# Down projection in two passes by halves of the features, with seven-product Strassen blocks for five of 32 K tile pairs per pass

## The chip, the cores and the metric

The kernel runs on one core of one Trainium2 chip. The metric is the device time of one execution in microseconds. A core has five engines that work beside each other, each with its own queue of instructions: TensorE (PE in the profile; PEld is its load of the stationary operand), VectorE (DVE), ScalarE (ACT), GpSimd (POOL) and SyncE (SP, which only issues DMAs here).

## The reference

One layer of a hybrid encoder block, 256 tokens of 2048 features in float32, one batch. The part that the change touches is the last line but one.

```python
proj = x @ w_in[l]
...
mix = jnp.concatenate([ret_out, mla_out], axis=-1) @ w_out[l]
x = _layer_norm(DEEPNORM_ALPHA * x + mix, ln1_g[l], ln1_b[l])
h = jnp.square(jax.nn.relu(x @ w_up[l])) @ w_down[l]     # (256, 8192) @ (8192, 2048)
x = _layer_norm(DEEPNORM_ALPHA * x + h, ln2_g[l], ln2_b[l])
```

## The kernel before

All large products keep float32 accuracy by splitting each operand into a high part, rounded to the type float32r, and a low part, the rest, and by three matmuls: high by high, high by low, low by high. For the weights, ACT casts the high part (L175) and DVE subtracts it for the low part (L176), 128x1024 elements at a time; such a piece is called a half tile here.

The weights come in `Job`s, in the order in which they are used: a load of 1 MB into one of three `raw` buffers (`NRAW`, on SP's queue) and pieces that split it into one of five slots (`NSLOT`). `unit()` is called after each group of matmuls and writes up to two further pieces into the queues of ACT and DVE (`next_piece`), as long as the slot five pieces back has been given back by `free`. A piece without a slot (`slotted` false) goes out as soon as its turn comes. The order in every queue is the order of these calls, as `manual_schedule` is set: nothing is reordered. Generators in `side` are stepped once per unit, ahead of the pieces.

The up projection goes over 64 feature tiles; `up_evac` squares the positive part into `rr` (8192 x 256, transposed, in SBUF). The down projection is `xstat`: the tokens are the stationary operand (two blocks `tb` of 128), the weights stream 512 columns at a time. Before the change its loop (L937 to L949) goes over K tiles `kt` of 128; all 2048 features of both token blocks accumulate in the eight PSUM banks `ad`. A K tile is 2 (token blocks) x 3 (parts) x 4 (banks) = 24 matmuls. `r_split(b)` makes high and low part of `rr` for four K tiles at a time (block b), into two buffers `rhl`, in the middle of the block before (L946). Two `row_job`s (ln1's gain and bias, `x1_piece`, L351) stand between the weights after K tiles 8 and 16; `last_residual` adds the residual of the last bank by two matmuls with the identity. Six K tiles are held back: four are split ahead into `slab` buffers (`staged_down`), and at the end each bank gets its last 18 matmuls by itself (`down_bank`, L976 to L991), while DVE adds the residual, takes the statistics and finishes the banks before.

Of the kernel before, what the change touches and what calls it, by code (L numbers as in the profile page):

```python
# [14 lines left out]
P = 128  # L15
D = 2048
# [15 lines left out]
HALF_PI = 1.5707963267948966  # L32
PI_LO = 3.1415925
NRAW = 3
NDOWN = 58
NSLOT = 5
X_AFTER = {0: (1, 1), 1: (2, 2), 3: (4, 4), 6: (8, 4), 10: (12, 4)}

# [13 lines left out]
class Job:  # L52


    def __init__(self, load, pieces, slotted):
        self.load = load
        self.pieces = pieces
        self.slotted = slotted
        self.emitted = 0
# [8 lines left out]
def kernel(  # L68
# [32 lines left out]
    def acc(name):  # L101
        return psum.tile([P, 512], F32, tag="acc", name=name)
# [19 lines left out]
    def next_piece(force):  # L122
        while state["job"] < len(jobs) and jobs[state["job"]].emitted == len(jobs[state["job"]].pieces):
            state["job"] += 1
        if state["job"] == len(jobs):
            return False
        job = jobs[state["job"]]
        if job.slotted:
            if len(holders) >= NSLOT and not force and not holders[-NSLOT][0]:
                return False  # L130
            holders.append(job.free[job.emitted])
        load_ahead(state["job"])
        job.pieces[job.emitted]()
        job.emitted += 1
        return True

    def use(job, n=None):
        while job.emitted < (len(job.pieces) if n is None else n):
            next_piece(True)
        return Cols(job.hi, job.width), Cols(job.lo, job.width)  # L140

# [9 lines left out]
    def weights(src, n, name, into=None, width=1024, cuts=None):  # L151

        job = Job(None, [], into is None)
        job.width = width
        spans = list(zip(cuts, cuts[1:])) if cuts else [(0, n)]

        def load():
            raw = raw_tile(job, f"raw_{name}")
            for i, (a, b) in enumerate(spans):
                (nc.scalar if name == "mla0" and i == 0 else nc.sync).dma_start(raw[:, a:b], src[:, a:b])  # L160

        def piece(i):
            a, m = i * width, min(width, n - i * width)
            if into is None:
                hi = wsp.tile([P, 1024], F32R, tag="hi", name=f"hi_{name}_{i}")
                lo = wsp.tile([P, 1024], F32R, tag="lo", name=f"lo_{name}_{i}")
            else:
                hi, lo = into(i)
            job.hi.append(hi)
            job.lo.append(lo)  # L170
            for o, e in spans if cuts else ((a, a + m),):
                o, e = max(o, a) - a, min(e, a + m) - a
                if o < e:
                    r = job.raw[:, a + o:a + e]
                    nc.scalar.copy(hi[:, o:e], r)  # L175
                    nc.vector.tensor_sub(lo[:, o:e], r, hi[:, o:e].bitcast(F32))  # L176
# [145 lines left out]
    def staged_down(i):  # L322
        def into(j):
            if (i // 2, "down") not in staged:
                staged[i // 2, "down"] = slab.tile([P, 8192], F32R, tag="slab", name=f"wst{2 + i // 2}")
            o = (2 * (i % 2) + j) * 2048
            t = staged[i // 2, "down"]
            return t[:, o:o + 1024], t[:, o + 1024:o + 2048]
        return into

    for half in range(2):
        row = []
        for i in range(KT // 2):
# [5 lines left out]
    j_up = [weights(w_up[ft], 2048, f"wu{ft}") for ft in range(64)]  # L339
    norm_rows = {}  # L340

    def row_job(i, pieces):
# [7 lines left out]
        op = nc.vector.tensor_mul if i == 0 else nc.vector.tensor_add  # L350
        op(c, c, norm_rows[i][:, a:a + 1024])  # L351

    down = {}
    for kt in range(NDOWN):
        down[kt] = weights(w_down[kt], 2048, f"wd{kt}")
        if kt in (8, 16):
            i = (8, 16).index(kt)
            row_job(i, [lambda i=i, tb=tb, a=a: x1_piece(i, tb, a) for tb in range(2) for a in (0, 1024)])
        if kt in (36, 41, 46, 51):
            i = (36, 41, 46, 51).index(kt)  # L360
            down[NDOWN + i] = weights(w_down[NDOWN + i], 2048, f"wd{NDOWN + i}", into=staged_down(i))
    for kt in (62, 63):
        down[kt] = weights(w_down[kt], 2048, f"wd{kt}")
    j_down = [down[kt] for kt in range(64)]
    row_job(2, [])
    row_job(3, [])

# [316 lines left out]

    xm = mid.tile([P, 5120], F32, tag="mid", name="xm")
    xt = xm[:, 0:2 * D].rearrange("p (b c) -> p b c", b=2)
    spare = xm[:, 2 * D:].rearrange("p (b i c) -> p b i c", b=2, i=4)
# [3 lines left out]
    def residual(tb, j, pb, st, with_stats=True):  # L691
        c = xt[:, tb, j * 512:(j + 1) * 512]
        if pb is not None:
            nc.vector.scalar_tensor_tensor(c, c, ALPHA, pb, op0=ALU.mult, op1=ALU.add)
        if with_stats:
            nc.vector.bn_stats(st[:, j], c)

    def out_steps(half, i):
        kp = (i + H // 2) % (KT // 2)
# [177 lines left out]

    rr = [slab.tile([P, 32, S], F32, tag="slab", name=f"rr{i}") for i in range(2)]

    def up_evac(ft, pb):  # L880
        t = work.tile([P, S], F32, tag="ut", name="ut", bufs=2)
# [5 lines left out]
    def last_residual(step):  # L887

        if step == 0:
            c = xt[:, 1, 3 * 512:]  # L890
            nc.vector.tensor_copy(identr, ident)
            nc.scalar.activation(mask, ident, AF.Copy, scale=-1.0)
            xb.append(work.tile([P, 2, 512], F32R, tag="xf", name="xb"))
            nc.scalar.activation(xb[0][:, 0], c, AF.Copy, scale=ALPHA)
            nc.vector.scalar_tensor_tensor(xb[0][:, 1], c, ALPHA, xb[0][:, 0].bitcast(F32),
                                           op0=ALU.mult, op1=ALU.subtract)
        else:
            for i in range(2):
                nc.tensor.matmul(ad[1][3], identr, xb[0][:, i], start=False, stop=False)

    xb = []
    rhls = {}

    def r_split(b):
        if b < 16:
            t = work.tile([P, 4, 512], F32R, tag="big", name="rhl", bufs=2)
            r = rr[b // 8][:, b % 8 * 4:b % 8 * 4 + 4]
            nc.scalar.copy(t[:, :, 0:S], r)
            nc.vector.tensor_sub(t[:, :, S:], r, t[:, :, 0:S].bitcast(F32))
            rhls[b] = t  # L910

    for ft in range(NSPLIT):
        up_evac(ft, first_pb[ft])
# [19 lines left out]
            unit()  # L933


    ad = [[(acc if j < 2 else bank)(f"d{tb}{j}") for j in range(4)] for tb in range(2)]
    for kt in range(NDOWN):  # L937
        hi, lo = use(j_down[kt])
        if kt == NDOWN - 2:
            r_split(15)  # L940
        for tb in range(2):
            xstat(ad[tb], [(rhls[kt // 4], kt % 4, hi, lo, 0)], (512,) * 4, kt == 0, False, tb)
            if tb == 1:
                free(j_down[kt])
            unit()
        if kt % 4 == 1 and kt // 4 < 14:  # L946
            r_split(kt // 4 + 1)
        if kt in (32, 36):
            last_residual((kt - 32) // 4)  # L949


    w_staged = []
    for kt in range(NDOWN, 64):
        hi, lo = use(j_down[kt])
        w_staged.append((rhls[kt // 4], kt % 4, hi, lo, 0))
    load_ahead(len(jobs))
    st2 = [stat.tile([P, 4, 6], F32, tag=f"ln{tb}", name=f"lm{tb}", bufs=1) for tb in range(2)]
    g2, b2 = norm_rows[2], norm_rows[3]

    def down_bank(tb, j):  # L960
        xstat(ad[tb], w_staged, (512,) * 4, False, True, tb, banks=(j,))

    def finish(tb, a, b):

# [11 lines left out]
    for j in range(4):  # L976
        down_bank(0, j)
        residual(0, j, ad[0][j], st2[0])
    stats(0, st2[0])

    shift = {j: (acc if j < 2 else bank)(f"sh{j}") for j in (1, 2)}
    for j in range(4):
        down_bank(1, j)
        finish(0, j * 512, (j + 1) * 512)
        if j < 3:
            residual(1, j, ad[1][j], st2[1])
        else:
            nc.vector.bn_stats(st2[1][:, j], ad[1][j])
        if j in shift:
            c = xt[:, 1, j * 512:(j + 1) * 512]  # L990
            nc.vector.tensor_mul(c, c, g2[:, j * 512:(j + 1) * 512])  # L991
# [5 lines left out]
    centred(1, 3, ad[1][3])  # L997
# [89 lines left out]
```

## Time and profile before

| what | value |
|---|---|
| median of three runs | 1133.36 us (1133.17 to 1133.53) |
| the profiled execution | 1133.73 us, span 1131.6 us |
| granted TensorE clock | 0.999 |
| busy: PE, DVE, ACT, POOL | 99%, 61%, 45%, 1% of the span |
| up projection, its loop | to about 773.5 us |
| down projection, first matmul | 773.7 us |
| last matmul of the down projection | 1122.1 us |
| r_split: ACT L908, DVE L909 | 16 each |
| HBM read | 214.12 MB |

The span is the time from the first to the last instruction in the profile; the execution's own time holds 2.1 us more. A row of a group gives the line, the engine, the operation, output<-inputs, the shape and the count, then the busy time in us and the mean of one in ns, then the idle time ahead of it and what ended it. A row of a timeline gives the start and the length in us; of a pair of operations merged in one row the length is from the first's start to the second's end. Line numbers are those of the kernel before.

### The profile page before, as it was taken

How to read it: one execution, taken by the hardware profiler on the slowest of the kernel's cores; microseconds unless marked ns; L12 is line 12 of the kernel's file. 1: busy time of each engine (PE TensorE's matmuls, PEld its weight loads, DVE VectorE, ACT ScalarE, POOL GpSimd, SP SyncE). 2: the span in 40 equal slices, each digit the busy share in tenths (PEclk: the TensorE clock that was granted, in tenths of full speed). 3: DMA queues.
4: the chain of work that ended last, by engine and by line, in shares of the span. 5: the costliest groups of instructions: out<-in, count | busy, mean ns of one | idle time of the engine just before them, and what ended most of it. 6: DMA issues, size and time to landing. Idle time of an engine off the chain costs nothing.

```text
span 1131.6 us, 14183 instructions
## 1 busy us (share of the span) xinstructions
PE 1123.8 (99%) x5648; PEld 956.2 (84%) x5648; DVE 689.5 (61%) x923; ACT 506.0 (45%) x653; POOL 10.0 (1%) x18
## 2 busy tenths in 40 slices
PE   9999999999999999999999999999999999999998
PEld 8888888888888889888888888888888888888886
DVE  6676775666656686555555655555656445555646
ACT  4445564545553545444444444444334444444520
POOL 0000000000000000000000000000000000000000
PEclk9999999999999999999999999999999999999999
DMA  8655374434475625555555555554566555666632
GB/s 296 234 203 177 125 248 149 165 142 179 153 281 185 233 103 206 195 191 190 187 186 186 187 189 188 188 193 173 192 229 235 199 186 188 226 237 240 225 112 74
DMA packets 34193, 217.12 MB, mean 192 GB/s; under 512 B 4176, under 2 KB 5200, under 8 KB 10704
## 3 DMA queue, kind: packets, MB, share of 16 engines
q1 hardware_dynamic: 33984, 215.97, 53.9%
q8 instruction: 44, 0.72, 0.2%
q10 hardware_dynamic: 144, 0.26, 0.1%
q14 instruction: 21, 0.17, 0.0%
HBM read 214.12 MB, written 2.10 MB: 191 GB/s over the span
## 4 chain that ended last, share of the span: by engine, by line
PE 98%; DVE 1%; ACT 0%; DMA 0%; POOL 0%; issue 0%; POOLq 0%; DVEq 0%; ACTq 0%
PE d L287 31%; PE up L613 20%; PE r L287 16%; PE up L619 10%; PE o L287 7%; PE m L287 4%; PE pu L613 2%; PE pv L287 1%; PE pu L619 1%; PE pq L287 1%; PE m L391 1%; PE up L782 1%; PE pms L644 0%; PE pms L643 0%; DMA raw_mla<-in_w_mla 0%; PE up L790 0%
## 5 line engine op out<-in xcount | busy, mean ns | idle before, releaser
L287 PE MATMUL d<-hi_wd,rhl 128*128 128x512 f32 x960 | 240.7, 389 | 0.0
L613 PE MATMUL up<-x1hl,hi_wu 128*128 128x512 f32 x984 | 234.8, 391 | 0.0
L176 DVE TENSOR_TENSOR lo_wd<-raw_wd,hi_wd 128x1024 fp32r<-128x1024 f32 x120 | 142.5, 1222 | 144.3 <-ACT hi_wd L175 144.1
L287 PEld LDWEIGHTS d<-hi_wd,rhl 128*128 128x128 f32 x960 | 180.2, 188 | 37.4
L613 PEld LDWEIGHTS up<-x1hl,hi_wu 128*128 128x128 f32 x984 | 180.8, 188 | 35.0
L175 ACT CAST hi_wd<-raw_wd 128x1024 fp32r<-128x1024 f32 x120 | 121.9, 1053 | 177.4 <-PE d L287 170.3
L176 DVE TENSOR_TENSOR lo_wu<-raw_wu,hi_wu 128x1024 fp32r<-128x1024 f32 x128 | 156.2, 1225 | 23.9 <-ACT hi_wu L175 19.7
L175 ACT CAST hi_wu<-raw_wu 128x1024 fp32r<-128x1024 f32 x128 | 134.4, 1055 | 31.4 <-PE up L613 28.2
L287 PE MATMUL r<-hi_ret,xhl 128*128 128x512 f32 x512 | 147.0, 397 | 0.0
L287 PE MATMUL d<-lo_wd,rhl 128*128 128x512 f32 x480 | 130.2, 389 | 0.0
L619 PEld LDWEIGHTS up<-x1hl,lo_wu 128*128 128x128 f32 x984 | 126.2, 191 | 4.8
L619 PE MATMUL up<-x1hl,lo_wu 128*128 128x256 f32 x984 | 127.7, 283 | 0.0
L287 PEld LDWEIGHTS r<-hi_ret,xhl 128*128 128x128 f32 x512 | 93.9, 188 | 18.2
L287 PEld LDWEIGHTS d<-lo_wd,rhl 128*128 128x128 f32 x480 | 90.1, 188 | 18.8
L883 ACT COPY ut<-up 128x256 f32<-128x256 f32 x64 | 23.9, 373 | 167.6 <-PE up L613 164.9
L884 DVE TENSOR_TENSOR ut<-ut,up 128x256 f32<-128x256 f32 x64 | 27.0, 422 | 113.1 <-ACT ut L883 113.1
L176 DVE TENSOR_TENSOR lo_ret<-raw_ret,hi_ret 128x1024 fp32r<-128x1024 f32 x64 | 75.7, 1220 | 23.8 <-ACT hi_ret L175 23.7
L287 PE MATMUL r<-lo_ret,xhl 128*128 128x512 f32 x256 | 79.4, 391 | 0.0
L175 ACT CAST hi_ret<-raw_ret 128x1024 fp32r<-128x1024 f32 x64 | 64.9, 1051 | 16.3 <-PE r L287 12.2
L287 PE MATMUL o<-hi_wo,mix 128*128 128x512 f32 x208 | 57.1, 392 | 0.0
L287 PEld LDWEIGHTS r<-lo_ret,xhl 128*128 128x128 f32 x256 | 48.0, 188 | 10.4
L287 PEld LDWEIGHTS o<-hi_wo,mix 128*128 128x128 f32 x208 | 38.7, 188 | 7.9
(200 smaller groups left out, 998.6 us busy)
## 6 DMA issues: line engine op xcount, KB each, us to landing
raw_wu<-in_w_up SPq DMA_DIRECT2D x64, 1024.0 KB, 4.8
raw_wd<-in_w_down SPq DMA_DIRECT2D x64, 1024.0 KB, 4.8
raw_ret<-in_w_ret SPq DMA_DIRECT2D x32, 1024.0 KB, 4.8
raw_wo<-in_w_out SPq DMA_DIRECT2D x16, 1024.0 KB, 4.8
raw_mla<-in_w_mla SPq DMA_DIRECT2D x14, 672.0 KB, 5.9
raw_qk<-in_w_qk SPq DMA_DIRECT2D x8, 640.0 KB, 3.9
row<-in_ln_rows SPq DMA_DIRECT2D x4, 1024.0 KB, 4.7
raw_uv<-in_w_uv SPq DMA_DIRECT2D x2, 1024.0 KB, 5.6
```

Source lines behind the costliest of these rows:

```text
L175: nc.scalar.copy(hi[:, o:e], r)
L176: nc.vector.tensor_sub(lo[:, o:e], r, hi[:, o:e].bitcast(F32))
L287: nc.tensor.matmul(accs[j][:, :w], x_part, w_part[:, a:a + w], start=first and fst and i == 0, stop=last and lst and i == len(steps) - 1)
L391: nc.tensor.matmul(am[tb][j][:, :w], xhl[:, kt, o + tb * P:o + (tb + 1) * P], w_part[:, j * 512:j * 512 + w], start=kt == 0 and fst and o ...
L613: nc.tensor.matmul(pb, hi[:, a:a + P], hl[:, k0 + i], start=first and i == ks[0], stop=last and i == ks[-1])
L619: nc.tensor.matmul(pb[:, 0:S], lo[:, a:a + P], hl[:, k0 + i, 0:S], start=False, stop=last and i == ks[-1])
L782: nc.tensor.matmul(pb[:, :, t], hi[:, k * P:(k + 1) * P], x1hl[:, k].rearrange("p (a t) -> p a t", a=2)[:, :, t], start=tb == 0 and k == 0 ...
L883: nc.scalar.copy(t, pb[:, S:])
L884: nc.vector.tensor_add(t, t, pb[:, 0:S])
```

## The change

The features are taken in two passes of 1024, so the accumulators `cb` take four banks (two token blocks, two banks), and the other four are free for partial products `mb`. The loop goes over 32 pairs of K tiles per pass; the number `n` below is the place in the pass. A load is now half the columns of two K tiles (still 1 MB; rows of 4 KB). `r_split` is called in both passes; pass 1 begins with blocks 14, 15, 11, 12, 13, whose parts are still there (the last three were put into the slab `sx`, `KEPT`).

In each pass five pairs (`SEVEN`: 3, 9, 15, 20, 25 and 2, 7, 12, 17, 22) are computed as a 2 x 2 block product after Strassen and Winograd: two token blocks by two K tiles, and two K tiles by two columns of 512. Seven products of three matmuls replace eight. Their operands are sums: `token_sums` (DVE, ACT, DVE) and `weight_sums` (four DVE operations of 512 columns, one of them in place in the raw tile), which go out as pieces without a slot ahead of the pair's four splits. Three products go to the accumulators directly, four accumulate in `mb` over the five pairs, and `add_sums`, a `side` generator, adds them to the residual `xt` in the right combinations after the fifth pair. The accumulators of pass 0 are added to `xt` at the start of pass 1 (`residuals`).

The two ln1 rows move into the up projection, after feature tiles 44 and 52. The last four pairs of pass 1 (eight half tiles) are held back; two of the pairs are split ahead, in the order of loads after pairs 24 and 26, into `sx`.

```diff
+ORDER = (tuple(range(16)), (14, 15, 11, 12, 13) + tuple(range(11)))
+SEVEN = ((3, 9, 15, 20, 25), (2, 7, 12, 17, 22))
+KEPT = {11: 0, 12: 1, 13: 2}
+NHELD = 4
+STAGE_AT = {24: 0, 26: 1}
...
-        if job.slotted:
+        if job.held:
+            return False
+        if job.slotted and job.emitted >= job.loose:
...
+    for ft in range(64):
+        j_up.append(weights(w_up[ft], 2048, f"wu{ft}"))
+        if ft in (44, 52):
+            i = (44, 52).index(ft)
             row_job(i, [lambda i=i, tb=tb, a=a: x1_piece(i, tb, a) for tb in range(2) for a in (0, 1024)])
...
+    def weights_pair(p, pair, into=None, seven=None):
...
+            nc.sync.dma_start(raw.rearrange("p (e c) -> p e c", e=2),
+                              w_down[2 * pair:2 * pair + 2, :, p * 1024:(p + 1) * 1024].rearrange("e p c -> p e c"))
...
+            nc.scalar.copy(hi[:, 0:n], src)
+            nc.vector.tensor_sub(lo[:, 0:n], src, hi[:, 0:n].bitcast(F32))
...
+        def token_sums():
...
+            nc.vector.tensor_add(st[:, 0], r0[:, P:], r1[:, P:])
+            nc.vector.tensor_sub(st[:, 1], st[:, 0], r0[:, 0:P])
+            nc.vector.tensor_sub(st[:, 2], r0[:, 0:P], r0[:, P:])
+            nc.vector.tensor_sub(st[:, 3], r1[:, 0:P], st[:, 1])
+            v = sums_of(seven)
+            nc.scalar.copy(v[:, :, 0], st)
+            nc.vector.tensor_sub(v[:, :, 1], st, v[:, :, 0].bitcast(F32))
+
+        def weight_sums():
...
+            nc.vector.tensor_sub(t1, b12, b11)
+            nc.vector.tensor_sub(t3, b22, b12)
+            nc.vector.tensor_sub(b12, b22, t1)
+            nc.vector.tensor_sub(t4, b21, b12)
...
+            job.loose = 2
+            job.pieces = [token_sums, weight_sums, lambda: split(0, job.raw[:, 1024:]),
+                          lambda: split(1, job.raw[:, 0:1024]), lambda: split(2, extra["t13"]),
+                          lambda: split(3, extra["t4"], 512)]
...
+    def add_sums(p, mb):
...
+        nc.scalar.copy(u, p1)
+        plus(0, 0, p1)
+        yield
+        nc.vector.tensor_add(u, u, p6)
+        nc.vector.tensor_add(v, u, p7)
+        yield
+        plus(0, 1, v)
+        nc.vector.tensor_add(v, v, p5)
+        yield
+        plus(1, 1, v)
+        nc.vector.tensor_add(u, u, p5)
+        yield
+        plus(1, 0, u)
...
+    def seven_products(p, pair, first, last):
...
+            for x_part, w_part, fst, lst in ((h, hi, True, False), (h, lo, False, False), (l, hi, False, True)):
+                nc.tensor.matmul(pb, x_part, w_part, start=alone and first and fst, stop=alone and last and lst)
+            if o or w == 3:
+                free(job, (w,))
+                unit()
+
+    for p in range(2):
+        cb = [[(acc, bank)[p](f"d{p}{tb}{j}") for j in range(2)] for tb in range(2)]
+        mb = None
+        for n, pair in enumerate(pairs[p][:32 if p == 0 else 32 - NHELD]):
+            b = pair // 2
+            if n in SEVEN[p]:
+                if mb is None:
+                    mb = [(bank, acc)[p](f"s{p}{j}") for j in range(4)]
+                seven_products(p, pair, n == SEVEN[p][0], n == SEVEN[p][-1])
+                if n == SEVEN[p][-1]:
+                    side.append(add_sums(p, mb))
+            else:
+                job = j_down[p][pair]
+                for e in range(2):
+                    hi, lo = use(job, e + 1)
+                    for tb in range(2):
+                        xstat(cb[tb], [(rhls[b], 2 * (pair % 2) + e, hi, lo, e * 1024)], (512, 512),
+                              n == 0 and e == 0, p == 0 and n == 31 and e == 1, tb)
+                        if tb == 1:
+                            free(job, (e,))
+                        unit()
+            if n % 2 == 0:
+                i = n // 2 + 1
+                if p == 0 and i < 16:
+                    r_split(ORDER[0][i], KEPT.get(ORDER[0][i]))
+                elif p == 1 and 4 <= i < 15 and ORDER[1][i + 0] not in KEPT:
+                    r_split(ORDER[1][i])
+        if p == 0:
+            side.append(residuals(cb))
+    r_split(ORDER[1][15])
...
+    for part in (slice(0, 4), slice(4, 8)):
+        for j in range(2):
+            down_bank(0, j, part)
+            if part.stop == 8:
+                residual(0, 2 + j, cb[0][j], st2[0], True)
+            elif j == 0:
+                gain(1)
     stats(0, st2[0])
...
+    down_bank(1, 0)
+    finish(0, 0, 512)
+    finish(0, 512, 1024)
+    residual(1, 2, cb[1][0], st2[1], True)
+    gain(2)
+    down_bank(1, 1)
+    finish(0, 1024, 1536)
+    finish(0, 1536, 2048)
```

More of the change, by code (lines that the diff above doesn't have):

```diff
@@ L58, in __init__ @@
         self.slotted = slotted
+        self.loose = 0
+        self.held = False
         self.emitted = 0
@@ L137, in use @@
     def use(job, n=None):
-        while job.emitted < (len(job.pieces) if n is None else n):
+        while job.emitted < (len(job.pieces) if n is None else job.loose + n):
             next_piece(True)
@@ new lines, in sums_of @@
+    def sums_of(q):
+        return extra["sx"][:, q * 1024:(q + 1) * 1024].rearrange("p (i h c) -> p i h c", i=4, h=2)
+    pairs = [[2 * b + i for b in ORDER[p] for i in range(2)] for p in range(2)]
+    j_down = [{}, {}]
+    for p in range(2):
+        for n, pair in enumerate(pairs[p]):
+            if p == 0 or n < 32 - NHELD:
+                j_down[p][pair] = weights_pair(p, pair, None, SEVEN[p].index(n) % 2 if n in SEVEN[p] else None)
+                if p == 1 and n in STAGE_AT:
+                    i = STAGE_AT[n]
+                    pair = pairs[1][32 - NHELD + i]
+                    j_down[1][pair] = weights_pair(1, pair, ((2, 3), (1, 0))[i])
+            elif n >= 32 - NHELD + 2:
+                j_down[p][pair] = weights_pair(p, pair)
@@ L365 @@
+    j_down[0][pairs[0][SEVEN[0][0]]].held = True
     row_job(2, [])
@@ L885, in up_evac, with r_split @@
         nc.vector.scalar_tensor_tensor(r, t, 0.0, t, op0=ALU.max, op1=ALU.mult)
[L887 to L896, printed above, removed]
-        else:
[L898 to L910, printed above, removed]
+    rhls = {}
+    def r_split(b, keep=None):
+        if keep is None:
+            t = work.tile([P, 4, 512], F32R, tag="big", name="rhl", bufs=2)
+        else:
+            t = extra["sx"][:, (keep + 1) * 2048:(keep + 2) * 2048].rearrange("p (k t) -> p k t", k=4)
+        r = rr[b // 8][:, b % 8 * 4:b % 8 * 4 + 4]
+        nc.scalar.copy(t[:, :, 0:S], r)
+        nc.vector.tensor_sub(t[:, :, S:], r, t[:, :, 0:S].bitcast(F32))
+        rhls[b] = t
     for ft in range(NSPLIT):
@@ L933 @@
             unit()
[L936 to L940, printed above, removed]
-        for tb in range(2):
[L942 to L949, printed above, removed]
+    extra["sx"] = slab.tile([P, 8192], F32R, tag="slab", name="sx")
@@ new lines, with col, plus @@
+    extra["t13"] = work.tile([P, 1024], F32, tag="xf", name="t13")
+    extra["t4"] = ut
+    j_down[0][pairs[0][SEVEN[0][0]]].held = False
+    st2 = [stat.tile([P, 4, 6], F32, tag=f"ln{tb}", name=f"lm{tb}", bufs=1) for tb in range(2)]
+    u, v = spare_flat[:, 0:512], spare_flat[:, 512:]
+    def col(tb, j):
+        return xt[:, tb, j * 512:(j + 1) * 512]
+    def add_sums(p, mb):
+        p1, p6, p5, p7 = mb
+        def plus(j, tb, src):
+            c = col(tb, 2 * p + j)
+            nc.vector.scalar_tensor_tensor(c, c, ALPHA, src, op0=ALU.mult, op1=ALU.add)
+        nc.scalar.copy(u, p1)
[11 more added lines that the diff above has]
+        plus(1, 0, u)
+        if p == 1:
+            c = col(1, 3)
+            nc.vector.tensor_copy(identr, ident)
+            nc.scalar.activation(mask, ident, AF.Copy, scale=-1.0)
+            xb = work.tile([P, 2, 512], F32R, tag="xf", name="xb")
+            nc.scalar.copy(xb[:, 0], c)
+            nc.vector.tensor_sub(xb[:, 1], c, xb[:, 0].bitcast(F32))
+            for _ in range(6):
+                yield
+            for i in range(2):
+                nc.tensor.matmul(cb[1][1], identr, xb[:, i], start=False, stop=False)
@@ new lines, in residuals @@
+    def residuals(old):
+        for tb in range(2):
+            for j in range(2):
+                residual(tb, j, old[tb][j], st2[tb], True)
+                yield
+    def seven_products(p, pair, first, last):
+        job = j_down[p][pair]
+        x, k, q = rhls[pair // 2], pair % 2 * 2, SEVEN[p].index(pairs[p].index(pair)) % 2
+        for a, w, o, pb, alone in ((("x", 1, 0), 0, 0, cb[0][0], False), (("s", 3), 0, 512, cb[0][1], False),
+                                   (("x", 0, 0), 1, 0, mb[0], True), (("s", 1), 1, 512, mb[1], True),
+                                   (("s", 0), 2, 0, mb[2], True), (("s", 2), 2, 512, mb[3], True),
+                                   (("x", 1, 1), 3, 0, cb[1][0], False)):
+            use(job, w + 1)
+            if a[0] == "x":
+                h, l = (x[:, k + a[1], i * S + a[2] * P:i * S + (a[2] + 1) * P] for i in range(2))
+            else:
+                h, l = (sums_of(q)[:, a[1], i] for i in range(2))
+            hi, lo = job.hi[w][:, o:o + 512], job.lo[w][:, o:o + 512]
+            for x_part, w_part, fst, lst in ((h, hi, True, False), (h, lo, False, False), (l, hi, False, True)):
[3 more added lines that the diff above has]
+                unit()
@@ new lines @@
+    for p in range(2):
+        cb = [[(acc, bank)[p](f"d{p}{tb}{j}") for j in range(2)] for tb in range(2)]
[8 more added lines that the diff above has]
+                    side.append(add_sums(p, mb))
+            else:
+                job = j_down[p][pair]
+                for e in range(2):
[14 more added lines that the diff above has]
+            side.append(residuals(cb))
@@ L952, with down_bank @@
+    r_split(ORDER[1][15])
     w_staged = []
-    for kt in range(NDOWN, 64):
-        hi, lo = use(j_down[kt])
-        w_staged.append((rhls[kt // 4], kt % 4, hi, lo, 0))
+    for pair in pairs[1][32 - NHELD:]:
+        hi, lo = use(j_down[1][pair])
+        w_staged += [(rhls[pair // 2], 2 * (pair % 2) + e, hi, lo, e * 1024) for e in range(2)]
     load_ahead(len(jobs))
-    st2 = [stat.tile([P, 4, 6], F32, tag=f"ln{tb}", name=f"lm{tb}", bufs=1) for tb in range(2)]
     g2, b2 = norm_rows[2], norm_rows[3]
-    def down_bank(tb, j):
-        xstat(ad[tb], w_staged, (512,) * 4, False, True, tb, banks=(j,))
+    def down_bank(tb, j, part=slice(0, 8)):
+        xstat(cb[tb], w_staged[part], (512, 512), False, part.stop == 8, tb, banks=(j,))
@@ L974, in centred, with gain @@
                                        op0=ALU.subtract, op1=ALU.mult)
[L976 to L991 removed]
+    def gain(j):
+        nc.vector.tensor_mul(col(1, j), col(1, j), g2[:, j * 512:(j + 1) * 512])
+    for part in (slice(0, 4), slice(4, 8)):
+        for j in range(2):
+            down_bank(0, j, part)
[3 more added lines that the diff above has]
+                gain(1)
+    stats(0, st2[0])
+    shift = {j: acc(f"sh{j}") for j in (1, 2)}
+    down_bank(1, 0)
[6 more added lines that the diff above has]
+    finish(0, 1536, 2048)
+    nc.vector.bn_stats(st2[1][:, 3], cb[1][1])
     for j in shift:
```

65 lines of the change are left out of this document (36 added, 29 removed).

## Prediction

> **What bounds the kernel now.** I read the busy shares and the chain that ended last on the page first, then the chain in order of time for the down projection, then this stage's engine shares, and last the groups and the engine timelines, for the order in which work queues.
>
> ```profile
> PE 1123.8 (99%) x5648; PEld 956.2 (84%) x5648; DVE 689.5 (61%) x923; ACT 506.0 (45%) x653; POOL 10.0 (1%) x18
> ...
> 773.91 201.28 PE d L287 x888
> ...
> 975.64 146.89 PE d L287 x648
> ...
> 774.00:1092.00 318.00, 318.00 (x1405) 263.31 (x1404) 173.89 (x151) 140.06 (x142) 0.00 (x0) 1.00 0.59 211
> ...
> ACT hi_wd L175 <- PE d L287: 170.3, 58, 3.9
> DVE lo_wd L176 <- ACT hi_wd L175: 144.1, 61, 3.5
> ```
>
> TensorE is busy for 99% of the span, and the chain runs through the down projection (d) without a gap: 888 + 648 = 1536 matmuls of 512 columns in 348.17 us, 0.2267 us each, at the full granted clock (the last 1.00 in the window's row). So a matmul less is 0.2267 us less, as long as nothing makes TensorE wait. The window's columns after its length are PE, PEld, DVE, ACT, POOL: DVE has 173.89 of 318 us of work (55%). The two waits say who sets the rhythm: ACT waits for TensorE to give back a weight slot, DVE waits for ACT. They are spare time, not bottlenecks. But what stands in a queue runs in the order written: where a layer-norm row's four operations stood behind one split of the weights, the next splits came only after them, from 818.35, though their slots were free before:
>
> ```profile
> 812.66 1.23 DVE L176 TENSOR_TENSOR lo_wd<-raw_wd,hi_wd 128x1024 fp32r<-128x1024 f32 x1 [1.94 <-ACT hi_wd L175]
> 813.80 4.62 DVE L351 TENSOR_TENSOR xm<-xm,row 128x1024 f32<-128x1024 f32 x4
> 818.35 3.49 DVE L176 TENSOR_TENSOR lo_wd<-raw_wd,hi_wd 128x1024 fp32r<-128x1024 f32 x3
> ```
>
> TensorE did not wait for that, as five slots of weights lie ahead of it. Of r there is less ahead: r_split of the next block of four K tiles is queued when the block in use is half done, and a block lasts half as long in each of two passes.
>
> **What is removed.** A standard pair (two K tiles, half of the features) takes 2 x 2 x 3 x 2 = 24 matmuls, a seven-product pair 7 x 3 = 21. Ten such pairs save 30 matmuls: 30 x 0.2267 = -6.80 us. The products accumulate three in a row into one bank; that this has no price of its own is shown by the one group here with that order, 36 in 8.16 us, also 0.2267:
>
> ```profile
> 110.66 8.16 PE pq L287 x36
> ```
>
> **What is added on ACT and DVE.** These are the prices.
>
> ```profile
> L176 DVE TENSOR_TENSOR lo_wd<-raw_wd,hi_wd 128x1024 fp32r<-128x1024 f32 x120 | 142.5, 1222 | 144.3 <-ACT hi_wd L175 144.1
> L175 ACT CAST hi_wd<-raw_wd 128x1024 fp32r<-128x1024 f32 x120 | 121.9, 1053 | 177.4 <-PE d L287 170.3 <-DMA raw_wd<-in_w_down 6.1 <-PE up L613 1.0
> L514 DVE TENSOR_TENSOR sT<-ps,ml 128x128 f32<-128x128 f32 x8 | 2.2, 281 | 0.0
> L272 DVE TENSOR_TENSOR t<-qkr,sin 128x512 f32<-128x512 f32 x8 | 5.5, 686 | 1.6 <-ACT qkr L483 1.6
> L351 DVE TENSOR_TENSOR xm<-xm,row 128x1024 f32<-128x1024 f32 x8 | 9.2, 1219 | 0.0
> ...
> 955.13 0.62 ACT L894 ACTIVATE xb<-xm 128x512 fp32r<-128x512 f32 x1
> ...
> 838.12 1.98 PE L287 MATMUL d<-hi_wd,rhl 128*128 128x512 f32 x8
> ...
> 838.77 2.01 ACT L175 CAST hi_wd<-raw_wd 128x1024 fp32r<-128x1024 f32 x2 [3.44 <-PE d L287]
> ...
> 839.86 2.36 DVE L176 TENSOR_TENSOR lo_wd<-raw_wd,hi_wd 128x1024 fp32r<-128x1024 f32 x2 [3.08 <-ACT hi_wd L175]
> ...
> 773.52 0.87 PEld L287 LDWEIGHTS d<-hi_wd,rhl 128*128 128x128 f32 x4
> ...
> 773.75 1.07 PE L287 MATMUL d<-hi_wd,rhl 128*128 128x512 f32 x4
> ...
> 1106.24 0.69 DVE L694 SCALAR_TENSOR_TENSOR xm<-xm,d 128x512 f32<-128x512 f32 x1 [2.66 <-PE d L287]
> 1106.96 0.69 DVE L696 BATCH_NORM_STATS2 lm<-xm 128x6 f32<-128x512 f32 x1
> ```
>
> Reading them: the second matmul at 838.12 (838.35) is the last to read the slot that ACT refills at 838.77, so a slot is taken 0.42 us after its last matmul's listed start; DVE starts 1.09 after ACT. Two tile operations of DVE take 2.36, not 2.44: independent ones start 0.08 before the former ends (1.14 apart; by the same overlap 0.61 for 512 columns and 0.20 for 128, an estimate), dependent ones 0.03 after, as the last two rows show. The weight load runs 0.23 ahead of its matmul.
>
> A seven-product pair adds on DVE: 1.5 more splits (1.22 + 0.69), four token sums of 128 columns and one subtraction (4 x 0.28 + 0.69), four weight sums (4 x 0.69): 6.5 us, 65 for ten. Two passes need eleven more r_split calls (27 against 16): 13.4. add_sums is 8 operations of 512 per pass: 11. Together 89 us, less the 9.2 of the row operations, which leave the stage: DVE goes from 55% to some 80% of it. ACT gets some 2.3 per seven-product pair, eleven r casts and two copies, about 36 us on 140, and waits for DVE more than it makes DVE wait. On average there is room; what decides is where the work stands in the queue.
>
> The token sums are the operations that this trace has least of: 0.28 is the row of two plain inputs with 128 columns, and the dearest alternative, a row at 0.40 with PSUM as a source, does not apply to inputs in SBUF; it would add 0.5 to each late split.
>
> **Five late splits of r.** Take pass 0, pair 9 (seven products), with zero at the first matmul of pair 6 and 12 matmuls = 2.72 per half tile. After pair 6's first half (listed end of slot use 2.49) the program queues, in this order on DVE: second half of pair 8, token_sums, then weight_sums, the first split of pair 9, and only then r_split of block 4, which pair 8 needs. ACT starts at 2.49 + 0.42 = 2.91, DVE at 4.00. The split takes 1.14 to the next start; four token sums 1.01 (two of them dependent); then DVE must wait for ACT's cast of the sums, as weight_sums stands behind it: 0.04 + 0.62 + 0.04, and the subtraction 0.61; weight sums 0.61 x 2 + 0.72 + 0.61; the split 1.14; r_split 1.22: it ends at 4.00 + 8.4 = 12.4. Pair 8 starts at 10.88; its fifth matmul is the first to use the low part, loaded at 10.88 + 0.91 - 0.23 = 11.56. TensorE loses 12.43 - 11.56 = 0.87. This holds wherever the pair three ahead is even and a split follows it: pass 0 pairs 3, 9, 15, 25 and pass 1 pair 17. Five times: +4.35. Nothing is given back later: TensorE has no other spare time. Bounds: 0 each if DVE gets there 0.9 us earlier; 1.8 each if the high part also waits (below). At the other five the split is queued at another time (20; 12 and 22 of pass 1) or there is none (2 and 7, whose r was kept): r_split then ends a microsecond and more early.
>
> **The end of pass 1.** Zero at pair 22's first product (4.76 long; pair 24 starts at 10.20). DVE runs from 1.28: pair 23 (two), pair 24 (two), the held pair 28 (two, needing no slot), pair 25's first half, then the r_split that pair 24 needs. Pair 25's load reuses the buffer that pair 23's second half leaves at 3.86, and lands 4.8 later:
>
> ```profile
> raw_wd<-in_w_down SPq DMA_DIRECT2D x64, 1024.0 KB, 4.8
> ...
> raw_qk<-in_w_qk SPq DMA_DIRECT2D x8, 640.0 KB, 3.9
> ...
> raw_uv<-in_w_uv SPq DMA_DIRECT2D x2, 1024.0 KB, 5.6
> ```
>
> So ACT has it at 8.8, DVE at 9.9, r_split ends at 12.25: 12.31 against a load due at 10.88, 1.43 late. Then add_sums' eight operations, the copy of the identity and xb (6.5 us) and six more half tiles and r_split (7 x 1.14) are queued ahead of pair 26: the last split ends at 26.07, its load was due at 21.53 + 0.91 - 0.23 = 22.21 (pair 26 starts at 10.20 + 2 x 5.44 and the two matmuls of the residual, 0.45). Total 3.92, the first 1.43 included. Lower end: if the load lands before ACT asks, DVE never idles and it is 2.8; upper 4.8, if the load takes the 5.6 of the slowest 1 MB row, or if the high part waits too. I take 3.9: the load is one of those that the 4.8 is the median of.
>
> **Costed at nothing.** add_sums of pass 0: the same count puts block 14's split at 16.17 against 16.32, covered by 0.15 us only. The boundary: four residuals (eight 512 operations, 5.3 us) run while no r_split is due, and pair 2's last splits end 0.3 us ahead of use. The rows of the first layer norm (8 x 1.22 and two 1 MB loads on SP's queue, ahead of the next weights) move into the up projection:
>
> ```profile
> 449.20 3.65 PE up L613 x16
> 454.77 3.65 PE up L613 x16
> ...
> 600.00:770.00 170.00, 170.00 (x975) 150.03 (x974) 101.12 (x124) 73.61 (x93) 0.00 (x0) 1.00 0.54 190
> ```
>
> A feature tile takes 5.57 us there and leaves DVE (101.12 of 170) 2.2 of it; four half tiles, 11 us, lie ahead, of which a row takes 4.6. The DMA share is 0.54. Without that cover a row would cost up to 4.6. Still 64 loads of 1 MB; rows are 4 instead of 8 KB: raw_qk's 5 KB rows land 640 KB in 3.9, as fast in proportion, and a load may take 5.4 before it counts. The ends: 144 held matmuls become 96, in the last 48 of which (10.9 us, two banks) DVE has thirteen operations of 512 columns, about 0.75 each with the statistics' wait of 1.2, and is done about 0.3 before TensorE. Before it was idle for 0.49 ahead of the last statistics, so what follows the last matmul stays:
>
> ```profile
> 1121.32 0.75 DVE L968 SCALAR_TENSOR_TENSOR xm<-xm,lnrs,row 128x512 f32<-128x512 f32 x1
> 1122.56 0.70 DVE L988 BATCH_NORM_STATS2 lm<-d 128x6 f32<-128x512 f32 x1 [0.49 <-PE d L287]
> ```
>
> **Sum.** -6.80 + 4.35 + 3.92 = +1.5 us on the profiled execution's 1133.73, that is 1135.2; the median of the runs is 0.37 lower, so **1134.8**.
>
> [...] TensorE went without a gap here, so no row shows what a gap does to its clock. [...]
>
> **Rivals.** (1) The queues keep up: no split is late, 1133.36 - 6.80 = 1126.6. For it: DVE's 55%. Against: the counts above are of queue order, not of shares. (2) Only one of the two groups comes: 1130.5 with the end alone, 1130.9 with the five alone; each five hang on 0.9 us in a chain of 9.5. (3) Slower by one mechanism: TensorE waits for the whole r tile, high and low, before a block's first matmul. Then every late split costs 0.91 more, the end 0.91 once, and block 14's split falls late by 0.75: 1134.8 + 4.5 + 0.9 + 0.8 = 1141.0. It decides as soon as the first matmul of a block is seen waiting for DVE. Nothing in the trace before shows either way, as no split was late; the two halves are written by two instructions, which speaks against it. (4) Slower by dearer pieces: token sums at 0.40, 1134.8 + 5 x 0.5 = 1137.3; the load of pair 25 at 5.6, 0.8 more; DVE at its full durations with no overlap (8 x 0.08 in each late split, 18 x 0.08 at the end, 4.6 together), 1139.4. Against it: the rows quoted.
>
> **How the numbers follow.** Forecast 0.56, own range 1132.5 (0.5 less in each late split) to 1137.2 (0.5 more); (1) 0.10; (2) 0.14; (3) 0.10; (4) 0.10. Within 0.2% of 1133.36, about what a measurement of this kernel can tell from no change, is 1131.1 to 1135.6. The forecast lies 0.38 within and 0.18 above; (1) and 0.10 of (2) are faster; (3) and (4) slower. The range 1129.8 to 1139.5 reaches from below the cheaper half of (2) to the dearest of (4) and leaves out (1) and (3).
>
> **What would show it.** 1506 matmuls of d at 0.2267; DVE at about 80% of the stage; TensorE's idle in five places of about 0.9 us, each ended by the DVE line of r_split, and two longer ones at pass 1 pairs 24 and 26; weight loads waiting on nothing else. Wrong if r_split is never what TensorE waits for, if gaps stand inside the seven products instead (weight sums late), or if matmuls in one bank space out.

## The result, and the profile after

| kernel | median | runs | ratio to the kernel before (95%) |
|---|---|---|---|
| before | 1133.39 us (1133.15 to 1133.68) | 15 | |
| changed | 1135.46 us (1134.82 to 1136.91) | 15 | 1.0019 (1.0012 to 1.0026) |

The change costs 2.1 us, and the forecast was 1134.8. The fifteen executions are of two kinds: ten with a mean granted clock of 0.999 or 1.000 took 1134.82 to 1135.73 (median 1135.1), five at 0.998 took 1135.79 to 1136.91 (1136.6); the kernel before has no such spread in these runs. The profiled execution is one of the five: 1136.37 us, a span of 1134.3.

The page's busy shares (engine, busy us, share of the span, instructions), two groups of its costliest and the median landing of the weight loads:

```profile
PE 1120.5 (99%) x5618; PEld 951.8 (84%) x5618; DVE 770.8 (68%) x1060; ACT 541.8 (48%) x696; POOL 10.0 (1%) x18
...
L297 PE MATMUL d<-hi_wd,rhl 128*128 128x512 f32 x672 | 185.8, 393 | 5.5 <-DVE rhl L969 4.7
...
raw_wd<-in_w_down SPq DMA_DIRECT2D x64, 1024.0 KB, 5.4
```

TensorE has 30 matmuls fewer (5618 against 5648), and its main group of the down projection now has an idle time in front of it, ended by r_split's DVE line (L969). The waits of TensorE (total, times, longest) in this stage; the one ended by `sx` is that of pair 25, whose r_split writes a block of `KEPT`:

```profile
PE d L297 <- DVE rhl L969: 4.7, 6, 2.2
...
PE d L297 <- ACT rhl L968: 0.8, 1, 0.8
PE d L297 <- DVE sx L969: 0.6, 1, 0.6
```

The engines in the stage and in the 5 us after the longest wait (columns after the length: PE, PEld, DVE, ACT, POOL busy, then the granted clock, the DMA share, GB/s):

```profile
774.00:1092.00 318.00, 311.93 (x1366) 255.89 (x1365) 244.18 (x282) 169.71 (x178) 0.00 (x0) 1.00 0.57 195
1091.50:1096.50 5.00, 4.95 (x15) 3.98 (x16) 2.51 (x3) 2.10 (x2) 0.00 (x0) 0.66 1.04 406
```

DVE is at 244.18 of 318 us, 77% (forecast 80%). TensorE got 311.93 of 318. From the start of the first matmul of the down projection to that of the last it takes 351.7 us (773.1 to 1124.8) instead of 348.4; the 1507 steps between its 1508 matmuls (1506 of products, two of the residual) would be 341.6 at 0.2267 each. So 10.1 us are lost, and the chain in order of time says where. Around pair 9 of pass 0 (start, us, what):

```profile
795.22 13.61 PE d L297 x60
808.86 1.06 ACT hi_wd L381
809.94 1.23 DVE lo_wd L382
811.17 0.21 DVE xm L389
...
812.13 0.63 ACT sx L394
...
812.78 0.69 DVE sx L395
813.48 0.60 DVE t L401
...
815.44 0.69 DVE ut L404
816.13 1.14 DVE lo_wd L382
817.27 1.15 DVE rhl L969
...
818.46 4.83 PE d L297 x20
823.28 1.36 PE d L1061 x6
```

This is the queue that the prediction counted, operation by operation: a split of pair 8, the token sums, the cast of the sums, the weight sums, a split of pair 9, and only then r_split. Five standard pairs after 795.22 take 27.2 us, so pair 9 (L1061, the first of the seven products) was due at 822.42 and starts at 823.28: 0.86 lost. Of this the list of waits shows some 0.57 as idle; the rest is a slower restart, as the 20 matmuls behind the split take 4.82 us (818.46 to 823.28) instead of 4.53. The chain leaves TensorE in the same way ahead of pairs 3, 15 and 25 and of pair 17 of pass 1 (0.87, 0.88, 0.86, 0.87), and nowhere else before pair 22 of pass 1. From there:

```profile
1065.25 1.37 PE d L1061 x6
...
1068.99 5.11 DMA raw_wd<-in_w_down
...
1074.20 1.06 ACT hi_wd L381
...
1076.51 1.14 DVE rhl L969
...
1089.23 1.14 DVE lo_wd L382
1090.36 1.15 DVE rhl L969
1091.51 0.04 issue
1091.55 33.64 PE d L297 x140
```

The load of pair 25 is on it, then splits and add_sums, and the last r_split ends at 1091.51. TensorE's own timeline from pair 22 to the last matmul, with the two late splits (last field: idle before and what ended it):

```profile
1065.09 0.39 PE L1061 MATMUL d<-hi_wd,rhl 128*128 128x512 f32 x1
...
1076.24 0.73 PE L297 MATMUL d<-hi_wd,rhl 128*128 128x512 f32 x2 [0.80 <-ACT rhl L968]
...
1077.70 1.19 PE L297 MATMUL d<-hi_wd,rhl 128*128 128x512 f32 x4 [0.25 <-DVE rhl L969]
...
1080.11 0.62 PE L297 MATMUL d<-lo_wd,rhl 128*128 128x512 f32 x2
...
1091.55 2.08 PE L297 MATMUL d<-hi_wd,rhl 128*128 128x512 f32 x4 [2.16 <-DVE rhl L969]
...
1124.79 0.39 PE L297 MATMUL d<-hi_wd,rhl 128*128 128x512 f32 x1
```

Pair 22's first matmul starts at 1065.09 here (a piece of the chain starts where the one before it ends, 0.16 later). From there the last r_split ends after 26.42 us (forecast 26.07). The matmul at 1080.11 is 59 steps of 0.2267, 13.37 us, behind it, and 15.02 have passed: the split that pair 24 waits for costs 1.65, its slower restart included as in the 0.87 above. The last matmul, at 1124.79, is 238 steps or 53.95 us behind it, and 59.70 have passed: 5.75 lost, 4.10 of them at pair 26. Four matmuls behind that wait take 2.08 us where elsewhere they take 1.07. This is the 0.66 in the window above: the trace has the clock at 0.50 from 1091.58 to 1094.99, and the eight matmuls in this stretch start 0.427 apart, which costs 8 x 0.20 = 1.60. So 2.50 are left for the late split itself. Sum: 5 x 0.87 + 1.65 + 2.50 + 1.60 = 10.1, all of it.

### The profile page after: what moved, and what is told of

It reads as the page before. It is cut to its first block, busy times and chain, and to the rows that moved or that the text cites. A ratio compares the mean times of both kernels' runs of the same rounds, so it can differ in the third digit from the quotient of the medians.

```text
span 1134.3 us, 14315 instructions
## 1 busy us (share of the span) xinstructions
PE 1120.5 (99%) x5618; PEld 951.8 (84%) x5618; DVE 770.8 (68%) x1060; ACT 541.8 (48%) x696; POOL 10.0 (1%) x18
## 4 chain that ended last, share of the span: by engine, by line
PE 92%; DVE 6%; ACT 1%; DMA 0%; issue 0%; POOL 0%; POOLq 0%; DVEq 0%; ACTq 0%
PE d L297 21%; PE up L682 20%; PE r L297 15%; PE up L688 10%; PE o L297 7%; PE m L297 4%; PE s L1061 2%; PE d L1061 2%; PE pu L682 2%; DVE lo_wd L382 2%; PE pv L297 1%; PE pu L688 1%; PE pq L297 1%; PE m L460 1%; ACT hi_wd L381 1%; DVE rhl L969 1%
## 5 line engine op out<-in xcount | busy, mean ns | idle before, releaser
L382 DVE TENSOR_TENSOR lo_wd<-raw_wd,hi_wd 128x1024 fp32r<-128x1024 f32 x124 | 149.3, 1223 | 66.6 <-ACT hi_wd L381 65.0
L297 PE MATMUL d<-hi_wd,rhl 128*128 128x512 f32 x672 | 185.8, 393 | 5.5 <-DVE rhl L969 4.7
L381 ACT CAST hi_wd<-raw_wd 128x1024 fp32r<-128x1024 f32 x124 | 129.0, 1052 | 104.7 <-PE d L297 75.7
L297 PEld LDWEIGHTS d<-hi_wd,rhl 128*128 128x128 f32 x672 | 126.5, 189 | 34.6 <-DVE rhl L969 7.3
L297 PE MATMUL d<-lo_wd,rhl 128*128 128x512 f32 x336 | 105.3, 391 | 0.0
L297 PEld LDWEIGHTS d<-lo_wd,rhl 128*128 128x128 f32 x336 | 63.4, 189 | 13.2
```

Source lines behind the costliest of these rows:

```text
L297: nc.tensor.matmul(accs[j][:, :w], x_part, w_part[:, a:a + w], start=first and fst and i == 0, stop=last and lst and i == len(steps) - 1)
L381: nc.scalar.copy(hi[:, 0:n], src)
L382: nc.vector.tensor_sub(lo[:, 0:n], src, hi[:, 0:n].bitcast(F32))
```

## Experiments

Theory A (queue order): TensorE waits because r_split stands behind other work in DVE's and ACT's queues; the seven products and the two passes have no cost of their own. Theory B (load): DVE has too much to do around a seven-product pair, and whatever is moved ahead only makes something else late. Theory C: the passes, their DMA rows of 4 KB or the matmul order cost time. For the longer executions: the clock falls after the 2.5 us wait (D).

**The splits first, everywhere.** r_split goes out at the start of the even pair, ahead of its matmuls, instead of at its end (`next_split` holds the lines taken out below). The identity matmuls of the last residual come six units later.

```diff
-            for _ in range(6):
+            for _ in range(12):
                 yield
...
         for n, pair in enumerate(pairs[p][:32 if p == 0 else 32 - NHELD]):
             b = pair // 2
+            if n % 2 == 0 and (True):
+                next_split(p, n)
...
-            if n % 2 == 0:
-                i = n // 2 + 1
-                if p == 0 and i < 16:
-                    r_split(ORDER[0][i], KEPT.get(ORDER[0][i]))
```

> All r_split calls moved from the end of an even pair to its start, ahead of the pieces of the sums, and the two matmuls of the last residual six units later; the work is the same. Queue theory (the time is lost because r_split stands behind the sums in DVE's queue, 5 x 0.87 us and 4.0 us at the end of pass 1, and TensorE's clock falls after the longest of these waits): all of it goes, TensorE waits for no r_split, and the median is 1133.4 - 6.8 = 1126.6 us (1126.2 to 1127.4). Load theory (DVE has too much work or the loads in 4 KB rows land too late, so that moving one operation only moves the wait to a split of weights): more than 1130 us, with TensorE waiting for lo_wd or hi_wd instead.

Measured: 1126.59 us (1126.53 to 1127.52, 5 runs) against 1133.28, ratio 0.9942 (0.9929 to 0.9954). The longest wait of TensorE in this kernel's list, and its stage:

```profile
PE sh L1157 <- ACT warm L1155: 1.4, 1, 1.4
```

```profile
774.00:1092.00 318.00, 318.00 (x1405) 263.51 (x1404) 246.14 (x284) 172.95 (x181) 0.00 (x0) 1.00 0.58 199
```

That wait belongs to the end of the kernel; none in the down projection is left, with the same work on DVE (246 us). Of the 6.80 us that the saved matmuls are worth, 6.7 come out: A, against B and C.

**Each group alone.** The same move only where `p == 0 or n < 22` (the five late splits), without the shift of the identity matmuls; and only where `p == 1 and n >= 22` (the end), with it.

> r_split moved to the start of the pair everywhere except from pair 22 of pass 1 on. Queue theory: the five waits of 0.87 us go, the end stays: 1135.5 - 4.35 = 1131.1 us (1130.4 to 1132.2), with the same spread from run to run as the changed kernel. Load theory: less than half of that, over 1133.3 us.

> r_split moved to the start of the pair only from pair 22 of pass 1 on, and the last residual's two matmuls six units later. Queue theory: the two waits at the end (4.0 us) and the slower matmuls behind the longer one go, the five stay: 1126.6 + 4.35 = 1130.95 us (1130.5 to 1131.5), with a spread of under 0.6 us between runs, as no wait is longer than 1 us. If the spread of the changed kernel has nothing to do with the long wait, it stays at about 2 us. Load theory: over 1133.3 us.

Measured, both beside the same runs of the kernel before (1133.28): with the five moved 1132.12 (1130.57 to 1132.99, 11 runs), ratio 0.9988 (0.9979 to 0.9997); with the end moved 1131.1 (1130.67 to 1131.79, 11 runs), 0.9981 (0.9972 to 0.999). The waits of TensorE, first with the five moved, then with the end moved:

```profile
PE d L297 <- DVE rhl L969: 2.4, 2, 2.2
...
PE d L297 <- ACT rhl L968: 0.9, 1, 0.9
```

```profile
PE d L297 <- DVE rhl L969: 2.3, 4, 0.6
...
PE d L297 <- DVE sx L969: 0.6, 1, 0.6
```

Each move removes its own group of waits and leaves the other as it was. The second came out at its number. The first is 1.0 us above its own: ten of its eleven executions had the clock of 0.998 and took 1131.43 to 1132.99 (median 1132.2), the one at 1.000 took 1130.57. By the terms above, 1133.28 - 6.80 + 1.65 + 2.50 = 1130.6 is due without the fall of the clock and 1132.2 with it. The long wait is in the first kernel and not in the second, whose executions are all at 0.999 or more; that bears out D but leaves open why the clock falls here ten times in eleven and in the changed kernel five times in fifteen. The spread of the second, 1.1 us where under 0.6 was expected, is not explained; the kernel before spread over 1.5 us on that chip.

**The passes without the seven products.**

```diff
-SEVEN = ((3, 9, 15, 20, 25), (2, 7, 12, 17, 22))
+SEVEN = ((), ())
```

The partial sums go with it; the last residual's identity matmuls are prepared after pair 12 of pass 1 instead.

> The two passes with all that belongs to them (4 KB rows, 27 r_split calls, eight held half tiles, ln1 rows in the up projection), but no seven-product pair: 1536 matmuls, no sums. Queue theory: the passes cost nothing by themselves, 1133.4 us (1133.1 to 1134.0). Rival: the passes cost 1 us or more, for the later landing of the loads or the residuals between the passes: 1134.4 or more, and then the seven products are worth more than their net shows.

Measured: 1133.5 (1132.83 to 1134.29, 11 runs), ratio 1.0001 (0.9992 to 1.001). By the interval the two passes, eleven more r_split calls, rows of 4 KB and the moved ln1 rows cost 1.1 us at most together. In the trace the down projection takes 348.4 us from its first matmul to its last (773.02 to 1121.41), as before the change. What is left of C, the matmul order, falls with the first experiment, and the cost of the change lies with the sums in the queue.

**More in the queue.** The changed kernel with one weight sum written twice, on DVE alone.

```diff
             nc.vector.tensor_sub(t3, b22, b12)
+            nc.vector.tensor_sub(t3, b22, b12)
```

> The changed kernel with the second weight sum written twice: 512 columns, 0.61 us more of DVE work in each of the ten seven-product pairs. Queue theory: only the five pairs with a late r_split behind them pay, 5 x 0.61 = +3.0 us, and perhaps 0.3 at pair 2 of pass 1: 1138.2 to 1139.2 us by the median of 1135.5. Load theory (all ten pay): +6.1, 1141.5 us. If DVE's sums were not on the path: no change.

Measured: 1139.64 (1139.47 to 1140.99, 5 runs), ratio 1.0061 (1.0048 to 1.0074), 4.2 us above the changed kernel, a little beyond the queue's range. The chain at pair 9:

```profile
815.19 0.61 DVE t L402
...
815.83 0.70 DVE t L403
...
816.56 0.70 DVE raw_wd L404
...
819.11 1.15 DVE rhl L970
...
820.30 3.74 PE d L297 x15
```

The operation that was to cost 0.61 costs 0.73 (815.83 to 816.56): it writes the tile of the one ahead and starts only after that one's end. The five places lose 0.73 to 0.75 more each, 3.7 together, and the chain shows 0.5 more within pair 2 of pass 1, where a weight split becomes late. The other four seven-product pairs lose nothing more. So the cost passes one for one through the five late splits and hardly elsewhere, as A has it; the size of the piece was wrong.

**The cover that was not named.** The first experiment with the identity matmuls left after six units.

> All r_split calls early, but the last residual's two matmuls where the change has them, six units after add_sums. Their second operand is ready 1082.9 us into the run of the kernel with all calls early, and by its matmuls TensorE would come to this place at 61.15 + 19.7 us after 1000, 1080.9. Queue theory: a new wait of about 1.9 to 2.1 us takes the place of the ones removed, 1126.6 + 2.0 = 1128.6 us (1128.2 to 1130.3, the upper part if the clock falls after it). If this place does not matter: 1126.6.

Measured: 1129.63 (1128.32 to 1130.56, 6 runs) against 1133.3, ratio 0.997 (0.9958 to 0.9982). TensorE's timeline near pair 24 of pass 1:

```profile
1080.01 0.61 PE L297 MATMUL d<-hi_wd,rhl 128*128 128x512 f32 x2
1082.09 1.01 PE L1039 MATMUL d<-xb,identr 128*128 128x512 f32 x2 [1.47 <-DVE identr L1031]
```

With r_split out of the way, the residual's operands (add_sums, then the identity's copy, on the same DVE queue) are what TensorE waits for next: 1.47 idle, and 2.0 with the slower restart, which is the new wait that was expected. In the changed kernel this was hidden by the late splits. This profile is of the shortest execution, 1128.32; the others took up to 2.2 us longer, two of them at a clock of 0.998, and no profile shows where.

**More products.** The first experiment with 13 and with 16 seven-product pairs instead of 10.

```diff
-SEVEN = ((3, 9, 15, 20, 25), (2, 7, 12, 17, 22))
+SEVEN = ((3, 7, 11, 15, 19, 22, 25), (2, 6, 10, 14, 18, 22))
...
+SEVEN = ((3, 6, 9, 12, 15, 18, 21, 24), (2, 5, 8, 11, 14, 17, 20, 22))
```

> As the kernel with all r_split calls early, with thirteen seven-product pairs instead of ten (3, 7, 11, 15, 19, 22, 25 and 2, 6, 10, 14, 18, 22). Queue theory: three pairs save 3 x 0.68 = 2.0 us, as DVE has 82% of the stage by the same prices and the queue has room: 1124.6 us (1124.3 to 1125.3). Rival (DVE's load decides after all): new waits eat it, 1126 us or more.

> The same with sixteen, every third pair (3, 6, ... 24 and 2, 5, ... 20, 22). DVE would need 14.5 of 15.6 us in each stretch of three pairs, and more than there is at the end of pass 1 with add_sums. If only the order in the queue decides: 1126.6 - 6 x 0.68 = 1122.5 us. If the load decides from here on: TensorE waits for DVE again, mostly in the second half of each pass, and it is slower than thirteen, 1125 us or more.

Measured: 13 pairs 1124.71 (1124.51 to 1124.97, 5 runs), ratio 0.9924 (0.9911 to 0.9936); 16 pairs 1124.42 (1123.8 to 1125.18, 5 runs), 0.9922 (0.9909 to 0.9936). Both beat both kernels, and they can't be told apart. Stages with 13 and then with 16 pairs, and the waits of TensorE with 16:

```profile
774.00:1092.00 318.00, 318.00 (x1405) 263.31 (x1404) 264.46 (x318) 180.08 (x192) 0.00 (x0) 1.00 0.58 201
```

```profile
774.00:1092.00 318.00, 317.23 (x1397) 261.63 (x1397) 281.67 (x351) 184.93 (x200) 0.00 (x0) 1.00 0.58 201
```

```profile
PE d L1061 <- DVE lo_wd L382: 0.4, 1, 0.4
PE d L297 <- DVE lo_wd L382: 0.4, 1, 0.4
```

Thirteen pairs take 9 matmuls away (2.0 us) and gain 1.9, with DVE at 83%. Sixteen take away 18 (4.1) and gain 2.2: the waits are now for splits of the weights, at the end of pass 1, with DVE at 89%. There theory B sets in, though neither of the two times expected for sixteen came (1122.5, or 1125 and more).

**How long a wait the clock stands.** Two kernels made from the one before: in eight feature tiles of the up projection (8, 11, ... 29) TensorE waits for a DVE subtraction of 256 to 2048 columns, and then adds its zeros to the sum by one more matmul. In the first this stands after four matmuls of the tile, in the second after eight, so the waits differ.

```diff
+GAPS = {8: 1, 11: 2, 14: 3, 17: 4, 20: 5, 23: 6, 26: 7, 29: 8}
...
+            nc.vector.tensor_sub(zero, r, r)
+            nc.tensor.matmul(pb, gap[0][:, 0:P], x1hl[:, 0], start=False, stop=False)
```

> The kernel before, with eight waits of TensorE of growing length put into the up projection (after feature tiles 8, 11, 14 ... 29, after four matmuls of the tile): a matmul by zeros, added into the bank, waits for a DVE subtraction of 256 to 2048 columns queued ahead of it. Waits of about 2.4 to 4.3 us, worked out from the DVE rows (evacuation to 1.55 us after the tile before, a split 1.2, then 0.16 and 0.27 per 256 columns, less the 0.9 of the four matmuls). Clock theory (a wait of about 2.6 us can put TensorE at half rate for some microseconds): behind some of these waits matmuls of 512 columns take 0.43 instead of 0.227 us for up to 3.4 us, behind the longest of them nearly always. Rival (the slow matmuls were work that arrived late, not the clock): they run at 0.227 behind every wait.

> The same with the waits after eight matmuls of the tile: about 1.5 to 3.3 us. Clock theory: full rate behind the waits of under 2 us, half rate behind some of those over 2.5. [...] Rival (any wait is followed by slow matmuls): slow behind all eight.

Measured, one execution each: 1173.55 and 1160.12 us. The waits on TensorE's timeline, three of the first kernel with the three windows behind them (PE busy, granted clock, DMA share, GB/s), then the shortest that dropped the clock in the second:

```profile
465.27 0.64 PE L930 MATMUL up<-x1hl,gap 128*128 128x512 f32 x1 [2.10 <-DVE gap L929]
...
527.88 0.50 PE L930 MATMUL up<-x1hl,gap 128*128 128x512 f32 x1 [2.90 <-DVE gap L929]
...
548.25 0.79 PE L930 MATMUL up<-x1hl,gap 128*128 128x512 f32 x1 [3.17 <-DVE gap L929]
```

```profile
465.30:470.30 5.00, 5.00 (x23) 0.66 0.00 0
...
527.90:532.90 5.00, 5.00 (x30) 1.00 0.13 18
548.20:553.20 5.00, 4.95 (x18) 0.50 0.00 0
```

```profile
560.87 0.62 PE L930 MATMUL up<-x1hl,gap 128*128 128x512 f32 x1 [2.53 <-DVE gap L929]
```

Over both kernels: the four waits of 1.20 to 2.00 us left the clock at 1.00. Of the seven from 2.10 to 2.90, four (2.10, 2.53, 2.63, 2.80) were followed by 0.50 to 0.66 and three (2.27, 2.37, 2.90) by 1.00. All five from 3.07 on were followed by 0.50 to 0.69. So a wait like that of pair 26, 2.16 in the list, can drop the clock and need not: D stands.

Length alone doesn't decide between 2.1 and 2.9, but the same two traces show another difference. The changes of the clock in a trace lie whole multiples of 3.413 us apart (in the first kernel at 465.48, 468.89, 506.44, 509.85, 547.40 and so on; in the changed kernel at 6.14, 1091.58, 1094.99 and 1132.53, which is 318, 1 and 11 steps), as on a grid, and the low clock is 0.50 for one step of it (3.41 us, six times) or two (6.83, three times). Divided at the grid, each of the nine waits that dropped the clock had 2.01 us or more within one step, and the clock fell at that step's end; of the seven others none had more than 1.94. So the 2.90, divided into 1.94 and 0.96, left the clock alone, and the 2.10, in one piece, dropped it. The wait of the changed kernel agrees (2.16 in one piece, with the fall at 1091.58). In the kernel with one more sum the longest wait in the list is 2.0, and the 140 matmuls of the chain behind it take 33.55 us, as against 33.64 in the changed kernel and 140 x 0.2267 = 31.7; how that wait lay to the steps is not shown. The grid lies otherwise to the program in each trace (the clock's first change comes 6.66 us after the start in the kernel before and 6.14 in the changed one); that the same wait at the same place is therefore divided in one execution and not in the next was not shown. By the same reading a wait of 3.07 isn't sure to drop the clock: divided in the middle it would leave 1.54 on each side, less than the 1.94 above (an estimate). This is read from the traces, no kernel was made to test it, and it doesn't say why the fall came ten times in eleven in one kernel.

## Why the prediction was right, point by point

**Saved matmuls, -6.80.** Held: the kernel with all splits early comes out at the kernel before less 6.7, and its stage is without a wait.

**Five late splits, 5 x 0.87.** Held in place and size: 0.86 to 0.88 at the five places named, none at the other five pairs. Moving them gains 3.3 us at the medians and 4.5 between the executions without the fall of the clock (1135.1 to 1130.57, the latter a single one).

**The end, 1.43 and 3.92 in all.** Held in place and mechanism, a little low in size: 1.65 and 4.15. The row it leaned on moved: the load of pair 25 took 5.11 and the median rose from 4.8 to 5.4, within the bound that was given, and the first r_split ended 12.56 after pair 22's start (forecast 12.25). That shorter rows land as fast in proportion the row of raw_qk did not show: 640 KB in 3.9 us is 6.2 for 1 MB, against 4.8. The second number was met in part by luck: the terms listed behind 12.25, 6.5 and 7 x 1.14, add up to 14.5 and so to 26.7, not to 26.07; in the run it was 13.86, as the sums and copies took 5.9 and not 6.5. ACT's cast stood behind that load, so the high part too came late at pair 24 (the 0.80 ended by ACT's line), which the forecast had only as a bound; it added nothing, as the low part came later still.

**Costed at nothing.** The kernel with the passes alone shows this, 1133.5 and a stage of the same length. add_sums of pass 0 made nothing late, with its 0.15 us of cover. At the tail DVE waited 0.40 ahead of the last statistics, before 0.49, where 0.3 was reckoned:

```profile
1125.21 0.70 DVE L1142 BATCH_NORM_STATS2 lm<-d 128x6 f32<-128x512 f32 x1 [0.40 <-PE d L297]
```

**The rivals.** (1) and (2) fall with the waits seen. (3) falls with the chain at pair 9: of the pair's 24 matmuls 20 come after the late split, so four had run on the high part alone. (4) falls with the prices: the token sums take 0.20 to 0.29 on that chain and not 0.40, the load of pair 25 took 5.11, and DVE's independent sums stand 0.60 apart where one takes 0.69 alone; the doubled sum, which writes the tile of the one ahead, added 0.73 to the queue. That a source in PSUM is what makes the 0.40 was not shown: `ps` of the row at 0.28 (L514) is a PSUM tile, as is `po` of the one at 0.404 (L549).

**What was wrong in it.** Nothing was added for the clock. The late split had the forecast size, 2.50, and in the profiled execution TensorE's clock was still at 0.50 for 3.41 us behind it, 1.60 us of slower matmuls; 1.5 us is the difference between the two kinds of executions. With the terms measured here the kind without the fall is due at 1133.39 - 6.80 + 4.35 + 4.15 = 1135.1 and the kind with it at 1136.7; their medians are 1135.1 and 1136.6. So of the 0.66 by which the result stands above the forecast some 0.35 is the clock (1135.1 to 1135.46) and 0.23 the end; the rest is rounding. That ten of the fifteen were spared the fall is no merit of the forecast. The traces show the fall behind a wait of 2.16 us here and behind four of 2.10 to 2.80 in the kernels with eight waits. The other gap is a cover that was not named: the late splits themselves hid the wait for the residual's operands. It cost nothing here, but whoever mends only the first loses 3 us of the 6.8 at the median, of which the trace shows 2.0.

## What to carry to other kernels

When a scheme trades matmuls for work on the engines that prepare operands, count where each new operation stands in their queues; an engine that is busy for 77% of a stage can still be late at five known places, and moving one operation a pair ahead was worth 9 us here. Put what many matmuls need (a split for a whole block) ahead of what only the next pair needs, and after each wait that is removed look for the next in the same queue. Go on adding such work only while no wait appears: here that was between 83% and 89% of VectorE.

## What the hardware showed that was not expected

The granted clock fell to 0.50 after a wait of TensorE of 2.10 us and stayed at 1.00 after one of 2.90, both in the first of the two kernels with eight waits. What differed in the traces of these two was how much of the wait lay within one step of 3.413 us, of which the times between the changes of the clock are multiples: 2.01 and more dropped the clock (nine waits), 1.94 and less did not (seven). The low clock then lasted one or two steps, 3.41 or 6.83 us; in the changed kernel one step cost 1.60 us, as the starts of matmuls of 512 columns went from 0.2267 to 0.427 apart. In the kernel with one more sum the operation of DVE that writes the tile of the one ahead of it took 0.73 us of the queue (815.83 to 816.56), where an independent one took 0.60 in the changed kernel (813.48).
